# A probability turn that writes DRAM once and reads it back four times, with a longer pause before its use

## The chip, the cores and the metric

The kernel runs on one core of a Trainium2 chip. The metric is the device time of one execution in microseconds (us): the median of three runs is 922.42 us, from 922.07 to 927.72. The core has five engines that run their own instruction streams and meet through semaphores: TensorE (PE in the profile, PEld for its weight loads), VectorE (DVE), ScalarE (ACT), GpSimd (POOL) and SyncE (SP). In this kernel SP issues the loads of weights and POOL issues, beside a few small loads, the DMAs that this change is about.

## What is computed

Two layers over 256 positions of width 2048. Each layer multiplies x by one wide input matrix, runs three groups of heads side by side, gates them with SiLU, multiplies by an output matrix and applies a layer norm to the scaled residual:

```python
h = x @ w_in                              # 2048 -> 6672 columns
y_a = chunk_band_attention(q, k, v, rel)  # 8 "chunk" heads of 128, softmax over the chunks seen so far, with a bias by distance
o_b = gla_chunk_recurrence(...)           # 4 heads of gated linear attention
y_m = memory_attention(m_q, mk, mv)       # 4 "memory" heads, softmax over 256 fixed memory tokens
y   = concat(y_a * silu(a_z), y_b * silu(b_z), y_m * silu(m_z))
x   = layer_norm(alpha * x + y @ w_out)
```

Both softmax groups need their probabilities twice: the softmax is taken along the free dimension (one query position in each of the 128 partitions), but the product with the values wants the keys in the partitions. So each head's probabilities are turned (transposed) in between. The change is in this turn and in how long the program waits after it.

## The kernel before

**The stream of pieces.** Nearly all matmul work is a product of x (or of the gated heads) with a weight matrix of 512 (or 388) columns. Such a group is cut in 8 pieces. Each piece is loaded by SP into a tile `raw` (`piece`, L129), split by ACT into a rounded high part `wh` (L117) and by DVE into the rest `wl` (L118), and multiplied by PE in 16 matmuls (`ws_group`, weights stationary) or 12 (`as_group`, activations stationary), all recorded at L95 and accumulated in `acc`. `raw`, `wh` and `wl` have four buffers each, so the loads run up to about four pieces ahead of PE. A layer goes through its groups in a fixed order; the one that matters is, from the middle of the layer on: values 2, AQ0, AK0, values 3, AQ1, AK1, MQ, BZ, AZ0, AZ1, MZ, then four groups WO of the output matrix.

**Heads between pieces.** Every head is a Python generator (`a_head` L516 for the eight chunk heads, `m_head` L546 for the four memory heads, `gla` L312 for linear attention). After each piece the program calls `tick` (L52), which advances a count (by 1, or by 0.76 after a piece of 388 columns) and steps at most one generator that is due. A `yield 7` says: go on with me seven pieces later. At most two generators are active while linear attention runs, three afterwards. So the order of PE and of SP is written out by the program: a head's own matmuls stand at a fixed place between two pieces. DVE, ACT and POOL get their order from a scheduler that works with estimated times; each engine then executes strictly in its order.

**A chunk head** starts by asking for the bias of the head two further on (`load_bias`, L830, an SP load into one of four `bias` buffers; the buffer is free when the head four earlier has added its bias, L524). Then PE multiplies q and k (rows `bk<-qk,qk`), DVE scales and adds the bias (L524) and finds the maxima (L529), ACT takes the exponential (L531), DVE normalises (L532, L534), and `turned` (L505) turns the result: DVE transposes blocks of 32 by 32 (L508), which leaves the blocks in the wrong partitions; POOL writes them to a DRAM tile `home` with four DMAs (L511), one for every 32 partitions, each in pieces of one block row (96 numbers, 384 bytes), and reads `home` back with one DMA (L512) into `pT`. Then comes `yield 7`; PE multiplies `pT` with the values (rows `bk<-pT,asv`), ACT copies the result out (L543), and after `yield 2` the generator ends. The memory heads use the same `turned` with 128 numbers (512 bytes) to a piece; after their own `yield 7` ACT and DVE split `pT` (L117, L118), and two pieces later PE multiplies it with the memory's values (rows `bk<-sc,mv`).

A DMA from POOL is an instruction in POOL's stream: a read of `home` waits there until the writes have landed, and all that stands behind it on POOL waits too.

At the end of a group of gates the program calls `finish` (L69), which steps the heads that the gates need without further pieces, if they are not yet done.

Of the kernel before, what the change touches and what calls it, by code (L numbers as in the profile page):

```python
# [36 lines left out]
def hybrid_trunk_kernel(  # L37
# [7 lines left out]
    pe, dve, act, pool, sp = nc.tensor, nc.vector, nc.scalar, nc.gpsimd, nc.sync  # L45
# [44 lines left out]
    def nm(s):  # L90
        uid[0] += 1
        return f"{s}_{uid[0]}"

    def mm(o, l, r, start, stop):
        pe.matmul(o, l, r, start=start, stop=stop, skip_group_check=True)  # L95

    def bank():
        return psa.tile([P, 512], F32, name=nm("bk"), tag="bk")

    def scratch(shape, dtype=F32):  # L100
        return sc.tile(shape, dtype, name=nm("sc"), tag="sc")

    def small(shape, tag, bufs=1):
        return sm.tile(shape, F32, name=nm(tag), tag=tag, bufs=bufs)
# [400 lines left out]
    def turned(dst, src, n):  # L505

        blocks = scratch([P, 4, n])
        dve.transpose(blocks.rearrange("p b (g j) -> p g b j", j=32), src.rearrange("p (g b j) -> p g b j", b=4, j=32))  # L508
        home = drm.tile([P, 4, n], F32, name=nm("home"), tag=f"home{n}")
        for a in range(4):  # L510
            pool.dma_start(home[:, a].rearrange("(b i) n -> i b n", b=4), blocks[a * 32:(a + 1) * 32])  # L511
        pool.dma_start(dst, home)  # L512

    SCALE = P ** -0.5

    def a_head(h, load_bias, bias, q, k, asv, y):  # L516

        if h + 2 < 8:
            load_bias(h + 2)
        pb = bank()  # L520
        mm(pb[:, 0:128], q[:, 0:128], k[:, 0:128], True, True)
        mm(pb[:, 128:384], q[:, 128:256], k, True, True)
        s = scratch([P, 384])
        dve.scalar_tensor_tensor(s, pb[:, :384], SCALE, bias[h], op0=ALU.mult, op1=ALU.add)  # L524
        mx = small([P, 2], "mx", 4)
        zs = small([P, 2], "zs", 4)
        own = (slice(0, 128), slice(128, 384))
        for t in range(2):
            dve.tensor_reduce(mx[:, t:t + 1], s[:, own[t]], AX.X, ALU.max, negate=True)  # L529
        for t in range(2):  # L530
            act.activation(s[:, own[t]], s[:, own[t]], AF.Exp, bias=mx[:, t:t + 1], accum_out=zs[:, t:t + 1])  # L531
        dve.reciprocal(zs, zs)  # L532
        for t in range(2):
            dve.tensor_scalar(s[:, own[t]], s[:, own[t]], zs[:, t:t + 1], None, op0=ALU.mult)  # L534
        pT = tp.tile([P, 4, 96], F32, name=nm("pT"), tag="pT")
        turned(pT, s, 96)
        yield 7
        po = bank()
        v0 = 528 + h * P
        pv, pov = pT.rearrange("p a (g j) -> p g a j", j=32), po[:, :256].rearrange("p (t a j) -> p t a j", t=2, j=32)  # L540
        mm(pov, asv[:, 0, v0:v0 + P], pv[:, 0:2], True, False)
        mm(pov[:, 1], asv[:, 1, v0:v0 + P], pv[:, 2], False, True)
        act.copy(y, po[:, :256])  # L543
        yield 2

    def m_head(h, q, mk, mv, y):  # L546
# [17 lines left out]
        for t in range(2):  # L564
            dve.tensor_scalar(s[:, t], s[:, t], zs[:, t:t + 1], None, op0=ALU.mult)
        pT = hd.tile([P, 4, 128], F32, name=nm("pT"), tag="qe" if h % 2 else "gb_")
        turned(pT, s.rearrange("p t m -> p (t m)"), 128)
        yield 7
        ph, pl = scratch([P, 2, 256], F32R), scratch([P, 2, 256], F32R)
# [199 lines left out]
    for l in range(L):  # L769
# [58 lines left out]
        def load_bias(h):  # L828
            bias[h] = hd.tile([P, 384], F32, name=nm("bias"), tag="bias", bufs=4)
            sp.dma_start(bias[h], relw[l, h])  # L830
# [9 lines left out]
        for half in range(2):  # L840
            values(2 + half)
            q = heads(G_AQ0 if half == 0 else G_AQ1)
            k = heads(G_AK0 if half == 0 else G_AK1)
            gens.append([a_head(half * 4 + h, load_bias, bias, q[:, h], k[:, h], asv, yraw[1 + half][:, h]) for h in range(4)])
            waiting.extend(gens[-1])
# [36 lines left out]
        for n in range(WO_N):  # L882
            if last:
                g, b = scratch([P, 512]), scratch([P, 512])
            else:
                both = per.tile([P, 2, 512], F32, name=nm("gb"), tag=f"yr{n}")
                g, b = both[:, 0], both[:, 1]
# [126 lines left out]
```

## Time and profile before

| | before |
|---|---|
| median of three runs | 922.42 us (922.07 to 927.72) |
| profiled execution, its own time | 922.5 us |
| its span in the trace | 920.7 us |
| PE busy | 909.6 us, 99% of the span |
| DVE, ACT, POOL busy | 65%, 53%, 10% |
| DMAs of a turn | 4 writes `home<-sc` of 48 or 64 KB, 1 read `pT<-home` of 192 or 256 KB |
| turns in the program | 16 of chunk heads, 8 of memory heads |

The 1.8 us between the profiled execution's time and its span lie outside the recorded instructions. In the profile, times are counted from the start of the span. "Idle before" names what an engine waited for last. PE has almost no idle time, so what moves the end of this program is the little that PE does wait, and any new wait.

### The profile page before, as it was taken

The numbers are of one execution on the slowest core, as the hardware profiler recorded it, in microseconds if no ns is written. First come the engines' busy times: TensorE is split into PE (matmuls) and PEld (weight loads), VectorE is DVE, ScalarE is ACT, GpSimd is POOL, SyncE is SP. The second block draws the span as 40 slices with busy tenths as digits, with TensorE's granted clock in tenths as the row PEclk, the third lists the DMA queues.
The fourth block names the chain that finished last, engine by engine and source line by source line (L and its number), as shares of the span: only waits on it lengthen the run. The fifth ranks groups of instructions, "written<-read, shape, count | busy, mean of one in ns | idle before, by whom it ended". The sixth has DMA issues, their size and how long they took to land.

```text
span 920.7 us, 14332 instructions
## 1 busy us (share of the span) xinstructions
PE 909.6 (99%) x5420; PEld 798.8 (87%) x5420; DVE 602.2 (65%) x845; ACT 488.7 (53%) x702; POOL 87.8 (10%) x169
## 2 busy tenths in 40 slices
PE   9999999999999999999999999999989999999997
PEld 7889998998888888888888899889878888888885
DVE  6764478656566576555587665985746676776566
ACT  6644475475455565434476445654734565654350
POOL 1000000012033030000000000001211230310000
PEclk9999999999999999999999999999999999999998
DMA  9965865558576586655774466555565775776652
GB/s 306 335 191 173 297 219 165 157 178 278 170 216 203 200 252 205 216 195 184 233 255 164 152 205 202 186 163 179 209 212 175 220 214 177 228 251 208 199 162 91
DMA packets 75989, 189.33 MB, mean 206 GB/s; under 512 B 9224, under 2 KB 33160, under 8 KB 75664
## 3 DMA queue, kind: packets, MB, share of 16 engines
q1 hardware_dynamic: 69120, 173.30, 57.7%
q0 software_dynamic: 6656, 14.86, 5.5%
q8 instruction: 42, 0.69, 0.3%
q10 hardware_dynamic: 144, 0.26, 0.1%
q14 instruction: 27, 0.22, 0.1%
HBM read 181.01 MB, written 7.34 MB: 205 GB/s over the span
## 4 chain that ended last, share of the span: by engine, by line
PE 90%; DMA 4%; ACT 2%; DVE 1%; issue 1%; POOL 1%; SPq 0%; POOLq 0%
PE acc L95 82%; PE bk L95 7%; DMA home<-sc 2%; DMA raw<-w 2%; DMA pT<-home 1%; ACT wh L117 1%; POOL home L511 1%; ACT sc L474 1%; PE bk L599 0%; DVE wl L118 0%; ACT L290 0%; PE bk L498 0%; ACT asv L807 0%; DVE mx L529 0%; DVE qk L263 0%
## 5 line engine op out<-in xcount | busy, mean ns | idle before, releaser
L118 DVE TENSOR_TENSOR wl<-raw,wh 128x1024 fp32r<-128x1024 f32 (+3 forms) x321 | 369.9, 1154 | 251.6 <-ACT wh L117 250.3
L117 ACT CAST wh<-raw 128x1024 fp32r<-128x1024 f32 (+3 forms) x321 | 318.9, 995 | 338.1 <-PE acc L95 231.8
L95 PE MATMUL acc<-x,wh 128*128 128x512 f32 x1248 | 397.1, 400 | 0.2 <-ACT wh L117 0.2
L95 PE MATMUL acc<-wh,x 128*128 128x512 f32 (+2 forms) x1236 | 356.5, 369 | 0.0
L95 PEld LDWEIGHTS acc<-x,wl 128*128 128x128 f32 x1248 | 234.7, 188 | 55.3
L95 PEld LDWEIGHTS acc<-wh,x 128*128 128x128 f32 x1236 | 227.0, 188 | 27.8 <-ACT wh L117 0.4
L95 PE MATMUL acc<-x,wl 128*128 128x256 f32 x1248 | 246.0, 278 | 0.0
L95 PE MATMUL acc<-wl,x 128*128 128x512 f32 (+2 forms) x618 | 228.0, 369 | 0.0
L95 PEld LDWEIGHTS acc<-x,wh 128*128 128x128 f32 x1248 | 192.6, 189 | 2.5 <-ACT wh L117 0.8
L95 PEld LDWEIGHTS acc<-wl,x 128*128 128x128 f32 x618 | 116.0, 188 | 15.0 <-DVE wl L118 0.8
L511 POOL DMA_DIRECT2D home<-sc x96 | 52.5, 554 | 336.6 <-DVE sc L508 333.5
L531 ACT ACTIVATE sc<-sc,mx 128x128 f32<-128x128 f32 (+1 forms) x32 | 14.3, 448 | 10.6 <-DVE mx L529 10.5
L512 POOL DMA_DIRECT2D pT<-home x24 | 13.4, 560 | 54.2 <-DMA home<-sc 49.8
L95 PE MATMUL bk<-pT,asv 128*128 128x256 f32 (+1 forms) x64 | 14.0, 342 | 4.2 <-DMA pT<-home 4.2
L95 PEld LDWEIGHTS bk<-pT,asv 128*128 128x128 f32 x64 | 11.7, 197 | 5.9 <-DMA pT<-home 4.6
L386 ACT ACTIVATE sc<-sc 128x512 f32<-128x512 f32 x12 | 7.6, 633 | 15.4 <-DVE sc L384 15.3
L508 DVE STREAM_TRANSPOSE sc<-sc 128x384 f32<-128x384 f32 (+1 forms) x24 | 14.9, 621 | 0.6
L118 DVE TENSOR_TENSOR x<-sc,x 128x512 fp32r<-128x512 f32 x20 | 13.3, 684 | 0.7 <-ACT x L117 0.7
L304 POOL DMA_DIRECT2D gwraw<-gate_w x6 | 3.1, 522 | 106.0 <-PE bk L587 105.1
L95 PE MATMUL bk<-qk,qk 128*128 128x128 f32 (+1 forms) x64 | 13.1, 326 | 0.0
L118 DVE TENSOR_TENSOR x<-res,x 128x512 fp32r<-128x512 f32 (+2 forms) x14 | 10.4, 764 | 4.0 <-ACT x L117 4.0
L524 DVE SCALAR_TENSOR_TENSOR sc<-bk,bias 128x384 f32<-128x384 f32 x16 | 8.7, 543 | 6.6 <-PE bk L95 6.5
(207 smaller groups left out, 566.3 us busy)
## 6 DMA issues: line engine op xcount, KB each, us to landing
raw<-w SPq DMA_DIRECT2D x214, 512.0 KB, 4.3
raw<-w SPq DMA_DIRECT2D x64, 388.0 KB, 3.5
raw<-w SPq DMA_DIRECT2D x83, 256.0 KB, 3.5
bias<-relw SPq DMA_DIRECT2D x16, 192.0 KB, 4.2
home<-sc POOLq DMA_DIRECT2D x64, 48.0 KB, 3.7
pT<-home POOLq DMA_DIRECT2D x16, 192.0 KB, 4.1
res<-xT SPq DMA_DIRECT2D x4, 512.0 KB, 5.0
res<-xn SPq DMA_DIRECT2D x1, 2048.0 KB, 8.2
```

The lines of the kernel that those rows point to most:

```text
L95: pe.matmul(o, l, r, start=start, stop=stop, skip_group_check=True)
L117: act.copy(hi, src)
L118: dve.tensor_tensor(lo, src, hi.bitcast(F32), op=ALU.subtract)
L304: pool.dma_start(raw[i * 16:i * 16 + 16], gate_w[l])
L386: act.activation(dd, dd, AF.Abs)
L474: act.activation(sq, on[par][:, g], AF.Square, scale=1.0 / math.sqrt(P), accum_out=ms[:, par * 4 + g:par * 4 + g + 1])
L508: dve.transpose(blocks.rearrange("p b (g j) -> p g b j", j=32), src.rearrange("p (g b j) -> p g b j", b=4, j=32))
L511: pool.dma_start(home[:, a].rearrange("(b i) n -> i b n", b=4), blocks[a * 32:(a + 1) * 32])
L512: pool.dma_start(dst, home)
L524: dve.scalar_tensor_tensor(s, pb[:, :384], SCALE, bias[h], op0=ALU.mult, op1=ALU.add)
L531: act.activation(s[:, own[t]], s[:, own[t]], AF.Exp, bias=mx[:, t:t + 1], accum_out=zs[:, t:t + 1])
```

## The change

The one DRAM tile `home` keeps its size, but its rows are now the source's rows, unturned, so one DMA writes it; the blocks change partitions on the way back, where four DMAs each fill 32 partitions of `pT`. The pause of the chunk heads (not of the memory heads) is nine pieces.

```diff
@@ turned
         home = drm.tile([P, 4, n], F32, name=nm("home"), tag=f"home{n}")
-        for a in range(4):
-            pool.dma_start(home[:, a].rearrange("(b i) n -> i b n", b=4), blocks[a * 32:(a + 1) * 32])
-        pool.dma_start(dst, home)
+        pool.dma_start(home, blocks)
+        for b in range(4):
+            pool.dma_start(dst[b * 32:(b + 1) * 32], home[:, b].rearrange("(a i) n -> i a n", a=4))
@@ a_head
         turned(pT, s, 96)
-        yield 7
+        yield 9
         po = bank()
```

In the changed kernel the write has line L510 and the reads L512. Three places show what the change does to the order of the engines. The heads of a layer are numbered from 0.

POOL, first layer, the turns of chunk heads 0 and 1 (`home_1792` and `home_2065`) and what stands between them; minus is before, plus is the changed kernel:

```order
-L511 DMA home_1792<-sc_1790 32x4x96 x4
-L512 DMA pT_1789<-home_1792 128x384
+L510 DMA home_1792<-sc_1790 128x384
+L512 DMA pT_1789<-home_1792 32x4x96 x4
 L656 MEMSET gbrow_4341 128x128
 L658 DMA gbrow_4341<-ln_g 16x128
 L658 DMA gbrow_4341<-ln_b 16x128
-L511 DMA home_2065<-sc_2063 32x4x96 x4
-L512 DMA pT_2062<-home_2065 128x384
```

Five DMAs in either case; the single one is now the write.

PE, first layer, group AQ1. Before, head 0's product with the values (`pT_1789`) stands behind the group's second piece, and head 2's q times k (`bk_2121`) behind the third:

```order
L95 MATMUL bk_2093<-pT_1789,asv_729 128x256 [waits DMASW2_49,DVE_49]
L95 MATMUL bk_2093<-pT_1789,asv_729 128x128
L95 MATMUL acc_2012<-x_447,wh_2098 128x512 [waits Activation_49]
...
L95 MATMUL acc_2012<-x_447,wl_2099 128x256 x2
L95 MATMUL bk_2121<-qk_1497,qk_1215 128x128 [waits PE_49]
L95 MATMUL bk_2121<-qk_1497,qk_1215 128x256
```

In the changed kernel head 2's q times k stands behind the second piece (where `pT_1789` stood), and `pT_1789` two pieces later, behind the group's fourth piece and ahead of the next one (`acc_2168`):

```order
L95 MATMUL acc_2012<-x_513,wh_2141 128x512 x2
L95 MATMUL acc_2012<-x_513,wl_2142 128x256 x2
L95 MATMUL bk_2162<-pT_1789,asv_729 128x256 [waits DMASW2_49,DMASW1_49,DMASW7_49,DMASW0_49,PE_49]
L95 MATMUL bk_2162<-pT_1789,asv_729 128x128
L95 MATMUL acc_2168<-x_277,wh_2170 128x512 [waits Activation_49]
```

The product waits for four DMAs (DMASW) in place of one. Head 3's q times k, which stood one piece behind head 2's, now stands two pieces behind `pT_1789`, four behind head 2's. Between a chunk head's q times k and its product with the values there stand nine pieces, where seven stood (counting pieces of 388 columns for less).

SP, first layer, loads of the same group. Before, the load of head 5's bias (`bias_2166`, which waits until DVE has added head 1's bias) stands behind the group's fourth piece:

```order
L830 DMA bias_2119<-relw 128x384
L142 DMA raw_2144<-w 128x1024 [waits DMAHW6_49,DVE_49]
L830 DMA bias_2166<-relw 128x384 [waits DVE_49]
L142 DMA raw_2194<-w 128x1024 [waits DMAHW7_49,Activation_49]
L142 DMA raw_2216<-w 128x1024 [waits DMAHW1_49,Activation_49]
```

In the changed kernel the same load (`bias_2213`) stands two pieces later:

```order
L830 DMA bias_2093<-relw 128x384
L142 DMA raw_2118<-w 128x1024 [waits DMAHW5_49,DVE_49]
L142 DMA raw_2140<-w 128x1024 [waits DMAHW6_49,DVE_49]
L142 DMA raw_2169<-w 128x1024 [waits DMAHW7_49,DVE_49]
L142 DMA raw_2191<-w 128x1024 [waits DMAHW1_49,DVE_49]
L830 DMA bias_2213<-relw 128x384 [waits DVE_49]
```

## Prediction, made before the result was known

> **What bounds the kernel now.** The first part of the page comes first: who is busy.
>
> ```profile
> PE 909.6 (99%) x5420; PEld 798.8 (87%) x5420; DVE 602.2 (65%) x845; ACT 488.7 (53%) x702; POOL 87.8 (10%) x169
> ```
>
> PE is idle for 920.7 - 909.6 = 11.1 us of the span. An edit that leaves the number of matmuls alone can win no more than these 11.1 us and whatever PE loses by running slow; everything else it does is hidden or a loss. The table of waits, for PE alone, says what the idle time is:
>
> ```profile
> PE bk L95 <- DMA pT<-home: 4.2, 2, 2.8
> PE bk L95 <- DVE eps L768: 1.1, 1, 1.1
> ```
>
> Two waits for turned probabilities take 4.2 us, the longer 2.8 us; the rest of the 11.1 us is the start and the end of the program. The timeline of PE shows which heads these are. First the first layer, heads 1 to 3, up to head 4's q times k; then the same end in the second layer:
>
> ```profile
> 196.72 0.82 PE L95 MATMUL bk<-qk,qk 128*128 128x128 f32 x4
> 200.16 0.81 PE L95 MATMUL bk<-pT,asv 128*128 128x256 f32 x4
> 203.60 0.82 PE L95 MATMUL bk<-qk,qk 128*128 128x128 f32 x4
> 207.04 0.82 PE L95 MATMUL bk<-qk,qk 128*128 128x128 f32 x4
> 218.84 0.81 PE L95 MATMUL bk<-pT,asv 128*128 128x256 f32 x4
> 225.08 0.81 PE L95 MATMUL bk<-pT,asv 128*128 128x256 f32 x4
> 230.08 0.92 PE L95 MATMUL bk<-pT,asv 128*128 128x256 f32 x4 [1.40 <-DMA pT<-home]
> 247.58 0.82 PE L95 MATMUL bk<-qk,qk 128*128 128x128 f32 x4
> ...
> 677.42 0.81 PE L95 MATMUL bk<-pT,asv 128*128 128x256 f32 x4
> 683.81 1.65 PE L95 MATMUL bk<-pT,asv 128*128 128x256 f32 x4 [2.78 <-DMA pT<-home]
> 702.63 0.81 PE L95 MATMUL bk<-qk,qk 128*128 128x128 f32 x4
> ```
>
> The late one is head 3 in both layers. Its product took 1.65 us the second time, twice what the others take, and the windows around it say why: PEclk, the granted clock, is 0.57 in the 4 us that follow the longer wait, and 1.00 on either side.
>
> ```profile
> 680.00:683.00 3.00, 1.03 (x7) 0.73 (x5) 1.09 (x1) 1.04 (x1) 0.00 (x0) 1.00 0.99 328
> 683.00:687.00 4.00, 3.19 (x10) 2.78 (x11) 0.13 (x1) 0.37 (x1) 0.00 (x0) 0.57 0.52 172
> 687.00:690.00 3.00, 3.00 (x19) 2.60 (x19) 0.25 (x1) 1.33 (x2) 0.00 (x0) 1.00 0.00 0
> ```
>
> **What the two waits cost together.** From 196.72 to 207.04 PE takes three equal steps of 3.44 us, each one piece and one head's products. From 218.84 to 225.08 are two pieces and one such product, 6.24 us, so a piece alone is 6.24 - 3.44 = 2.80. In the first layer head 3's product was due at 225.08 + 3.44 = 228.52 and came at 230.08, 1.56 late; its row is 0.92 instead of 0.81, so 0.11 more. From there to head 4's q times k is 247.58 - 230.08 = 17.50, undisturbed 17.39. An undisturbed stretch from head 2's product to head 4's q times k is then 3.44 + 17.39 = 20.83. It took 22.50 in the first layer, 1.67 too long, and 702.63 - 677.42 = 25.21 in the second, 4.38 too long (2.95 late, 1.43 for the half clock). Together **6.05 us**.
>
> **Why head 3 is late.** POOL's timeline:
>
> ```profile
> 203.43 2.21 POOL L511 DMA_DIRECT2D home<-sc  x4 [12.61 <-DVE sc L508]
> 208.59 0.56 POOL L512 DMA_DIRECT2D pT<-home  x1 [2.94 <-DMA home<-sc]
> 212.66 2.18 POOL L511 DMA_DIRECT2D home<-sc  x4 [3.50 <-DVE sc L508]
> 218.92 0.56 POOL L512 DMA_DIRECT2D pT<-home  x1 [4.08 <-DMA home<-sc]
> 219.47 2.18 POOL L511 DMA_DIRECT2D home<-sc  x4
> 226.60 0.56 POOL L512 DMA_DIRECT2D pT<-home  x1 [4.95 <-DMA home<-sc]
> ```
>
> Head 3 began on PE one step behind head 2 (207.04 against 203.60), but a turn holds POOL for 219.47 - 212.66 = 6.81 us, most of it waiting for the writes to land. Head 3's first write has no idle time before it: it queued behind head 2's read.
>
> **The DMAs turned about: 0.** The page's list of DMA issues (KB each, then us to landing):
>
> ```profile
> home<-sc POOLq DMA_DIRECT2D x64, 48.0 KB, 3.7
> pT<-home POOLq DMA_DIRECT2D x16, 192.0 KB, 4.1
> home<-sc POOLq DMA_DIRECT2D x32, 64.0 KB, 4.1
> pT<-home POOLq DMA_DIRECT2D x8, 256.0 KB, 5.2
> ```
>
> One issue on POOL is 2.21 / 4 = 0.55, by either row. A chunk head's turn was: last of four writes issued after 3 x 0.55, landed after 3.7, read landed after 4.1: 9.45 us. It becomes one write of 192 KB, then three issues, then the last of four reads of 48 KB. Nothing in the trace writes 192 KB to `home` or reads 48 KB from it, so I take the same sizes in the other direction: 4.1 + 1.65 + 3.7 = 9.45. POOL is held as long as before, in another order: 0.55 and the wait, then four issues. Lower and upper bounds of the two unknown landings, by the fastest and the slowest of all turn DMAs:
>
> ```profile
> DMA to landing us min/median/max: 1.9/3.8/5.6
> ```
>
> That makes a turn 1.9 + 1.65 + 1.9 = 5.45 to 5.6 + 1.65 + 5.6 = 12.85 us, 4.0 shorter to 3.4 longer. What covers the longer end is weighed next, head by head.
>
> **The pause of nine pieces: -6.05 us.** Two more pieces give every chunk head 2 x 2.80 = 5.6 us. The worst was 2.95 late, so even with nothing else changed it has 5.6 - 2.95 = 2.65 us to spare. But head 3 also starts later: head 2 moves one step up, to 200.16; head 0's product follows two pieces later (200.16 + 3.44 + 2.80 = 206.40) and head 3 two more pieces on, near 212.6. It is then some 12.4 us behind head 2 where it was 3.44, more than the 6.81 that a turn holds POOL, so it no longer queues. Heads 1 and 2 are now one step apart and head 2 queues behind head 1; it had its product at 225.08, two us after its read should have landed (218.92 + 4.1 = 223.0), and the 5.6 us cover 6.81 - 3.44 = 3.4 of queueing. So I expect no wait for `pT` by a chunk head, even at the 3.4 longer turn for most of them, and without a wait no half clock. What is late next on PE: nothing that the wait table shows; the pieces.
>
> **Weights: 0.** SP's stream moves too. Before, SP stood still ahead of AQ1's fifth piece, because the bias of head 5 needs DVE's L524 of head 1:
>
> ```profile
> 185.27 0.34 SPq L142 DMA_DIRECT2D raw<-w  x1
> 198.55 0.33 SPq L830 DMA_DIRECT2D bias<-relw  x1
> 203.25 1.05 ACT L117 CAST wh<-raw 128x1024 fp32r<-128x1024 f32 x1 [1.35 <-DMA raw<-w]
> 207.51 0.81 PE L95 MATMUL acc<-x,wh 128*128 128x512 f32 x2
> ```
>
> That fifth piece was rounded at 203.25 + 1.05 = 204.30 and used at 207.51: 3.2 us of cover, the thinnest place of the stretch. The bias load now stands two pieces later in SP's order while head 1's L524 stays where it was, so SP stands still for less and the cover grows. If DVE's new order (head 2's softmax sits closer to head 1's) ate that cover, each us beyond 3.2 would be a us of PE.
>
> **Memory heads: 0.** Their pause is the same. The last two of the first layer:
>
> ```profile
> 343.87 0.76 DVE L118 TENSOR_TENSOR sc<-pT,sc 128x256 fp32r<-128x256 f32 x2 [0.24 <-ACT sc L117]
> 349.66 0.88 PE L95 MATMUL bk<-sc,mv 128*128 128x256 f32 x6
> ```
>
> `pT` is split at 344.63 and used at 349.66: 5.0 us of cover against at most 3.4. ACT and DVE would stand behind a late `pT` and hold up the next pieces, which have some us of cover of their own.
>
> **Three more semaphores for each product: 0.** Sixteen products now wait for four DMAs. In the step from 200.16 the product waited for a DMA and for DVE, and the step is 3.44, the same as that of q times k, so a further wait has no visible price. The nearest row for an upper end is a whole product of four matmuls in 0.81, 0.2 each: 16 x 3 x 0.2 = 9.6 us if each wait cost as much as a matmul. I take 0, as that step shows, and keep part of it in the range.
>
> **The sum.** 922.5 (the profiled execution's own time, 0.1 from the median) - 6.05 = **916.5 us**, 0.7% less. A difference under 1% is about what a measurement of this kernel can't tell from none.
>
> **A rule that speaks against part of it.** The Trainium skill, "TensorE: Matmul & The Clock Gate", section "HAM oscillation — how this bites in real kernels", says that only idle gaps above some 3.4 us make the clock drop. By that rule a 2.8 us wait has no such cost, the half clock has another cause and stays, and the sum is that of the first rival below. The trace speaks against it: the clock is 0.57 only in the 4 us behind the longest wait, and behind the 1.40 us wait the product took 0.92, not 1.65.
>
> **The rivals.**
> 1. *The half clock is not the wait's and stays.* Then only the lateness goes: 6.05 - 1.43 = 4.6, 917.9 us. For it: the shorter wait had none. Against it: the place. 0.07.
> 2. *A wait stays or a new one comes,* for `pT`, for the semaphores or for AQ1's weights, and takes part of the gain: 917.9 to 922.5. For it: the pauses shift every head's DVE and ACT work against the pieces. Against it: 2.65 and 3.2 us of cover. 0.11.
> 3. *Slower: the four reads run one after another.* If the reads of a turn don't overlap, the last lands after 4.1 + 4 x 3.7 = 18.9 in place of 9.45. The memory heads have 5.0 us of cover; 9.45 - 5.0 = 4.4 late, once for each pair, four pairs, each with a half clock of 1.43: 4 x 5.9 = 23.5, so 916.5 + 23.5 = 940 us. It decides from 5.0 us of extra landing, and outweighs the gain from 6.5 (4 x 1.5 = 6). Against it: four writes, issued 0.55 apart, let POOL go on 4.08 us after the last issue ended, so these overlapped. With smaller extra landings, 922.5 to 931: 0.05; beyond 931.7: 0.05.
> 4. *More than 1% faster.* That needs 9.2 us out of 11.1 of idle time and the half clock; the start and end are not touched. 0.02.
>
> **How the numbers follow.** The forecast, 916.5 with 0.8 on either side, has 0.70. 915.5 to 922.0 adds rival 1 and nearly all of rival 2, and leaves out some 0.15 above and 0.03 below. Faster by over 1%: 0.02; within 1%: 0.70 + 0.07 + 0.11 + 0.05 = 0.93; slower by over 1%: 0.05.
>
> **What would show it.** The two rows `PE bk L95 <- DMA pT<-home` are gone from the table of PE's waits; PE's idle time is near 6.9 us; the clock is 1.00 through the second layer's AK1; the single write lands in some 4 us and POOL's reads show no long wait but the first; SP's wait at L830 shrinks from 12.9. It is wrong if PE waits for `pT` again, if `acc` rows wait for ACT or DVE by more than a few tenths of a us, or if the `sc<-pT` casts wait several us each.

## The result, and the profile after

| | before | after |
|---|---|---|
| median of six runs each | 923.15 us (922.07 to 927.72) | 916.58 us (916.03 to 917.06) |
| profiled execution, its own time | 922.5 us | 916.47 us |
| its span | 920.7 us | 914.7 us |

The ratio after to before is 0.992, with a 95% interval of 0.990 to 0.994: a gain of 0.8% by the ratio and of 0.7% by the two medians. It lies within the 1% named above, and still the interval is clear of no change. The changed kernel's six runs lie within 1.0 us of each other; those of before within 5.7.

The page of the changed kernel, its first part:

```profile
span 914.7 us, 14341 instructions
...
PE 907.3 (99%) x5420; PEld 797.9 (87%) x5420; DVE 601.3 (66%) x845; ACT 492.2 (54%) x706; POOL 87.8 (10%) x169
```

PE is idle for 914.7 - 907.3 = 7.4 us, where it was idle for 11.1. Its table of waits (us in total, times, longest) has no row for `pT` any more, and begins so (what follows is 0.3 us and less):

```profile
PE bk L95 <- DVE eps L768: 1.1, 1, 1.1
PE acc L95 <- ACT wh L117: 0.6, 2, 0.3
```

PE's timeline, first from head 1's q times k to head 4's in the first layer, then the end of the same stretch in the second layer:

```profile
196.83 0.81 PE L95 MATMUL bk<-qk,qk 128*128 128x128 f32 x4
200.27 0.82 PE L95 MATMUL bk<-qk,qk 128*128 128x128 f32 x4
206.50 0.81 PE L95 MATMUL bk<-pT,asv 128*128 128x256 f32 x4
212.73 0.82 PE L95 MATMUL bk<-qk,qk 128*128 128x128 f32 x4
224.53 0.81 PE L95 MATMUL bk<-pT,asv 128*128 128x256 f32 x4
227.98 0.81 PE L95 MATMUL bk<-pT,asv 128*128 128x256 f32 x4
239.78 0.81 PE L95 MATMUL bk<-pT,asv 128*128 128x256 f32 x4
246.01 0.82 PE L95 MATMUL bk<-qk,qk 128*128 128x128 f32 x4
...
690.46 0.81 PE L95 MATMUL bk<-pT,asv 128*128 128x256 f32 x4
696.69 0.82 PE L95 MATMUL bk<-qk,qk 128*128 128x128 f32 x4
```

Every product takes 0.81 and none has idle time before it. Head 4's q times k comes at 246.01 where it came at 247.58, and in the second layer at 696.69 where it came at 702.63: 5.94 us earlier, of the 6.0 us by which the span is shorter. The 4 us of the second layer that ran at a clock of 0.57 now run at 1.00:

```profile
683.00:687.00 4.00, 4.00 (x25) 3.48 (x24) 2.89 (x3) 1.66 (x3) 0.00 (x0) 1.00 0.55 201
```

POOL's timeline, the turns of heads 1, 2 and 3 in the first layer (one write and four reads each):

```profile
205.33 0.56 POOL L510 DMA_DIRECT2D home<-sc  x1 [14.86 <-DVE sc L508]
207.79 2.19 POOL L512 DMA_DIRECT2D pT<-home  x4 [1.89 <-DMA home<-sc]
210.93 0.56 POOL L510 DMA_DIRECT2D home<-sc  x1 [0.95 <-DVE sc L508]
216.30 2.17 POOL L512 DMA_DIRECT2D pT<-home  x4 [4.80 <-DMA home<-sc]
218.46 0.56 POOL L510 DMA_DIRECT2D home<-sc  x1
222.42 2.17 POOL L512 DMA_DIRECT2D pT<-home  x4 [3.39 <-PE acc L95]
```

Head 3's write still has no idle time before it: it queues behind head 2's reads. How long it queues, DVE's rows for head 3's transpose tell, first in the kernel before, then in the changed one:

```profile
216.28 0.58 DVE L508 STREAM_TRANSPOSE sc<-sc 128x384 f32<-128x384 f32 x1
```

```profile
217.31 0.58 DVE L508 STREAM_TRANSPOSE sc<-sc 128x384 f32<-128x384 f32 x1
```

Before, the blocks were ready at 216.86 and the first write began at 219.47, 2.6 us later (3.1 in the second layer); now they are ready at 217.89 and the write begins at 218.46, 0.6 us later (0.3). Head 3's last read is issued by 222.42 + 2.17 = 224.59 and its product comes at 239.78, 15.2 us later. The list of DMA issues (KB each, median us to landing):

```profile
home<-sc POOLq DMA_DIRECT2D x16, 192.0 KB, 2.7
pT<-home POOLq DMA_DIRECT2D x64, 48.0 KB, 4.0
```

By these medians, a chunk head's turn is 2.7 + 3 x 0.55 + 4.0 = 8.35 us where it was 9.45. A single landing can differ much from the median: head 2's write in the first layer took 5.1 us.

### The profile page after: what moved, and what is told of

Same layout as the page of the kernel before. It is cut to its first block, busy times and chain, and to the rows that moved or that the text cites. A ratio compares the mean times of both kernels' runs of the same rounds, so it can differ in the third digit from the quotient of the medians.

```text
span 914.7 us, 14341 instructions
## 1 busy us (share of the span) xinstructions
PE 907.3 (99%) x5420; PEld 797.9 (87%) x5420; DVE 601.3 (66%) x845; ACT 492.2 (54%) x706; POOL 87.8 (10%) x169
## 4 chain that ended last, share of the span: by engine, by line
PE 98%; DMA 1%; SPq 0%; DVE 0%; ACT 0%; issue 0%
PE acc L95 90%; PE bk L95 7%; DMA raw<-w 1%; PE bk L599 0%; PE bk L498 0%; SPq L165 0%; SPq L178 0%; PE bk L397 0%; SPq L180 0%; ACT res L755 0%; ACT wh L117 0%; DVE stats L740 0%; PE bk L344 0%; DVE res L739 0%; DVE res L691 0%
## 5 line engine op out<-in xcount | busy, mean ns | idle before, releaser
L512 POOL DMA_DIRECT2D pT<-home x96 | 52.4, 553 | 56.7 <-DMA home<-sc 24.3
L510 POOL DMA_DIRECT2D home<-sc x24 | 13.4, 560 | 358.4 <-DVE sc L508 352.9
L632 DVE SCALAR_TENSOR_TENSOR res<-res,acc 128x512 f32<-128x512 f32 x15 | 9.7, 684 | 5.1 <-PE acc L95 5.1
```

The lines of the kernel that those rows point to most:

```text
L510: pool.dma_start(home, blocks)
L512: pool.dma_start(dst[b * 32:(b + 1) * 32], home[:, b].rearrange("(a i) n -> i a n", a=4))
L632: dve.scalar_tensor_tensor(r, r, ALPHA, acc, op0=ALU.mult, op1=ALU.add)
```

## The experiments

**Is it the pause or the turned DMAs?** First the pause alone, with the DMAs of before, then the DMAs alone, with the pause of seven.

```diff
-        yield 7
+        yield 9
```

> The pause of nine pieces alone; the turn writes DRAM four times and reads it once, as before. Theory 'the pause does it all': no wait of PE for pT, 6.0 us less than the kernel before, 916.5 us, as the full change. Theory 'the turned DMAs have a share': PE still waits for pT somewhere, or the time lies above the full change by 1 us or more, 917.5 to 920. If three more semaphores at each product cost PE something, this kernel (one semaphore) is faster than the full change, by up to 9.6 us; I expect 0.

Measured: 916.66 us (916.08 to 916.98, ten runs), ratio 0.993 (0.990 to 0.996). PE has no wait for `pT`. The pause alone gives the whole gain. It also prices the four semaphores of a product: with one DMA to wait for the kernel takes 916.66, with four 916.58, so the three further waits cost nothing that can be measured.

```diff
-        for a in range(4):
-            pool.dma_start(home[:, a].rearrange("(b i) n -> i b n", b=4), blocks[a * 32:(a + 1) * 32])
-        pool.dma_start(dst, home)
+        pool.dma_start(home, blocks)
+        for b in range(4):
+            pool.dma_start(dst[b * 32:(b + 1) * 32], home[:, b].rearrange("(a i) n -> i a n", a=4))
```

> The turned DMAs alone, with the pause of seven pieces. 'The pause does it all': head 3 stays late in both layers, 922.5 us, within 0.7 of the kernel before. 'The turned DMAs have a share': the profile of the full change has the 192 KB write landed after 2.7 us and the 48 KB reads after 4.0, so a turn takes 2.7 + 1.65 + 4.0 = 8.35 in place of 9.45; 1.1 us come off the lateness in each layer (1.56 and 2.95), 920.3 us, and 918.9 if the half clock goes with it.

Measured: 924.21 us (919.96 to 932.47, twelve runs), ratio 1.001 (0.998 to 1.004). The turned DMAs alone are worth nothing that these runs can tell: the interval reaches from 0.2% faster to 0.4% slower. This kernel's PE waits for `pT` in the same two places as before, the second time for 3.7 us instead of 2.8; first its row of waits, then POOL's rows for head 3, first layer:

```profile
PE bk L95 <- DMA pT<-home: 5.1, 2, 3.7
```

```profile
219.95 0.56 POOL L510 DMA_DIRECT2D home<-sc  x1
224.88 2.18 POOL L512 DMA_DIRECT2D pT<-home  x4 [4.37 <-DMA home<-sc]
```

The reads may start at 224.88, 1.7 us sooner than the one read of before (226.60), but there are four of them: the last has been issued at 224.88 + 2.18 = 227.06, against 226.60 + 0.56 = 227.16. What the single write saves ahead of the wait, three more issues take behind it. In the second layer the reads start only 0.3 us sooner (678.68 against 679.01), so the last is issued 1.3 us later (680.86 against 679.57), and the product is later too.

**How much pause is needed?** Eight and six pieces, with the DMAs of before, and eleven in the changed kernel.

```diff
-        yield 7
+        yield 8
```

> A pause of eight pieces, DMAs as before. Two reasons for the gain are told apart by the size: the pause gives each head 2.80 us a piece, and it moves the places where heads start. By the first alone head 3 of the second layer stays 2.95 - 2.80 = 0.15 us late and the first layer is on time: 916.7. If the starts matter, PE's order decides: here head 3's q times k stands three pieces behind head 2's where it stood one behind, so it does not queue on POOL, has several us of cover, and the time is again 916.5, with no wait for pT at all in the table.

Measured: 916.73 us (916.09 to 917.38, ten runs), ratio 0.993 (0.991 to 0.995). One more piece is enough. POOL and PE of this kernel, head 3 in the first layer:

```profile
217.20 2.21 POOL L511 DMA_DIRECT2D home<-sc  x4
223.65 0.56 POOL L512 DMA_DIRECT2D pT<-home  x1 [4.25 <-DMA home<-sc]
```

```profile
234.34 0.81 PE L95 MATMUL bk<-pT,asv 128*128 128x256 f32 x4
```

Head 3 still queues on POOL (no idle time before its write), but from the end of its read's issue, 224.21, to its product are 10.13 us. In the kernel before, it had 228.52 - 227.16 = 1.36 until its product was due. Of the 8.8 us more, 2.8 are the further piece; 3.0 come from head 3's later place (its q times k at 210.07, where it was at 207.04), and 2.95 from POOL, whose queue ahead of head 3 ends sooner (the read is issued by 224.21 instead of 227.16), since head 2 has moved up a step (its q times k at 200.40, where it was at 203.60).

```diff
-        yield 7
+        yield 6
```

> A pause of six pieces, DMAs as before: heads 1, 2 and 3 then start one step (3.44 us) apart and queue on POOL, 6.81 us each. Head 3's read should land some 4 us after its place on PE, in both layers. If a wait of that length halves the clock for 3.4 us, each layer loses 4 + 1.4 us over an undisturbed 916.5: 927.3 us, with the granted clock under 1 behind the wait in both layers. If the half clock of the kernel before was not the wait's, it shows in none or at another place, and the time is near 924.5.

Measured: 933.26 us (931.41 to 936.03, four runs), ratio 1.011 (1.007 to 1.016). Slower, as expected, by more than expected (927.3). Five products wait; PE's rows for them:

```profile
225.10 0.92 PE L95 MATMUL bk<-pT,asv 128*128 128x256 f32 x4 [1.07 <-DMA pT<-home]
231.50 0.92 PE L95 MATMUL bk<-pT,asv 128*128 128x256 f32 x4 [2.68 <-DMA pT<-home]
683.04 0.92 PE L95 MATMUL bk<-pT,asv 128*128 128x256 f32 x4 [1.19 <-DMA pT<-home]
689.64 1.03 PE L95 MATMUL bk<-pT,asv 128*128 128x256 f32 x4 [2.90 <-DMA pT<-home]
762.05 1.62 PE L95 MATMUL bk<-pT,asv 128*128 128x256 f32 x4 [2.94 <-DMA pT<-home]
```

The windows behind the three long waits (granted clock third from the end of a row):

```profile
232.00:237.00 5.00, 5.00 (x21) 4.29 (x21) 0.00 (x0) 0.81 (x2) 0.00 (x0) 0.66 0.42 142
...
690.00:694.00 4.00, 4.00 (x16) 3.46 (x15) 0.00 (x0) 0.37 (x1) 0.00 (x0) 0.57 0.48 170
...
762.00:766.00 4.00, 3.95 (x14) 3.42 (x15) 1.25 (x2) 0.79 (x2) 1.12 (x2) 0.57 0.79 264
```

A drop of the clock follows each wait of 2.68 us and more and none of the two shorter ones. The expectation had counted on the heads that were late before; the wait at 762.05 is that of another, later head, which had no wait at seven pieces.

```diff
-        yield 9
+        yield 11
```

> The full change with a pause of eleven pieces. If all of the gain is the wait that went, two pieces more are worth nothing: 916.6 us. If a longer pause makes the memory heads or the last gates late, PE waits there and the time is above 917.5.

Measured: 916.46 us (916.12 to 916.78, four runs), ratio 0.992 (0.991 to 0.994): the same as with nine. Beyond eight pieces nothing more is to be had.

**Is it the queue on POOL that made head 3 late?** The kernel before, with its pause of seven, but with head 3 alone begun later:

```diff
     def a_head(h):
+        if h == 3:
+            yield 2
```

> Kernel before, with one edit: chunk head 3 of each layer starts two pieces later. Its pause and that of all others stays at seven pieces, the DMAs stay as before. Theory 'head 3 was late because it queued on POOL behind head 2': the queue (6.81 - 3.44 = 3.4 us) is gone, head 3 is on time, no wait for pT, 916.6 us. Theory 'seven pieces are too short for a turn': head 3 waits as before, 922.5.

Measured: 917.32 us (916.35 to 917.78, four runs), ratio 0.993 (0.992 to 0.995). Nearly the whole gain, without a longer pause for any head. POOL of this kernel, head 3 in the first layer:

```profile
218.85 2.20 POOL L511 DMA_DIRECT2D home<-sc  x4 [1.37 <-DVE sc L508]
```

Its first write now waits for DVE's transpose and not for POOL. Its q times k starts 6.4 us later than in the kernel before (213.40 against 207.04), and its first write all the same 0.6 us earlier (218.85 against 219.47). Seven pieces suffice for a head that does not queue; the lateness was that of one head that began one step behind another.

**What do the turned DMAs do for the memory heads?** The memory heads' pause is shortened to five pieces, in the changed kernel and in the kernel with the pause of nine and the DMAs of before.

```diff
     def m_head(h):
...
-        yield 7
+        yield 5
```

> The full change, and the memory heads' pause cut from seven pieces to five, 5.6 us less. It takes the cover away that hides the turned DMAs there. In the profile of the full change the second parts of the probabilities were ready 4.1 to 10.3 us ahead of the product that uses them; less 5.6 leaves one head 1.5 late and one 0.1: 918.2 us. If the four reads were much slower than one, more heads would wait, above 920.

> The same cut of the memory heads' pause, with the chunk heads' pause of nine pieces and the old DMAs (four writes, one read). With these DMAs the parts were ready 5.5 to 9.9 us ahead; less 5.6 leaves two heads 0.1 late: 916.8 us. If the DMAs turned about cost or save nothing, this and the kernel with turned DMAs and the same pauses lie within 1 us of each other; if turned DMAs are slower for the memory heads, this one is faster by 1 to 3 us.

Measured: 919.61 us (918.61 to 919.82, four runs), ratio 0.996 (0.994 to 0.997), with the turned DMAs; 927.64 us (925.13 to 930.65, eight runs), ratio 1.005 (1.003 to 1.007), with those of before. The first expectation missed by 1.4 us, the second by 11. Here, where the cover has been cut away, the kernel with the turned DMAs is 8.0 us the faster one. With the turned DMAs the shorter pause costs 919.61 - 916.58 = 3.0 us: in the profiled execution PE is idle for 0.9 us more and busy for 2.4 us more than in the changed kernel, without a drop of the clock. Row by row, PE is 0.4 us behind the changed kernel from the start of the program on, where the clock rose 1.0 us later, and loses another 2.8 around the four pairs of memory heads. PE's waits, first with the turned DMAs, then with those of before:

```profile
PE bk L95 <- ACT sc L117: 1.0, 2, 0.5
```

```profile
PE bk L95 <- ACT sc L117: 6.2, 3, 3.1
PE bk L95 <- DVE sc L118: 1.6, 2, 0.8
```

POOL's timelines for the first two memory heads of the first layer, turned DMAs first; the first row of each is the second head's write or writes, the next the first head's read or reads:

```profile
298.04 0.56 POOL L510 DMA_DIRECT2D home<-sc  x1 [2.01 <-DMA home<-sc]
298.83 2.21 POOL L512 DMA_DIRECT2D pT<-home  x4 [0.23 <-issue]
```

```profile
297.75 2.18 POOL L511 DMA_DIRECT2D home<-sc  x4 [0.32 <-DVE sc L508]
301.72 0.56 POOL L512 DMA_DIRECT2D pT<-home  x1 [1.79 <-DMA home<-sc]
```

With the DMAs of before, the first head's read stands behind the second head's four writes, 2.18 us of POOL, and starts 2.9 us later. But POOL had issued these writes by 299.93 and was then idle for 1.79 us, until writes had landed: it was not the issue of the four writes that held this read. Nor is the read what PE waited for here. It landed 4.0 us after its issue, at 305.7, and ACT's casts of it began at 308.45, without idle time, behind the cast of a piece:

```profile
308.45 1.33 ACT L117 CAST sc<-pT 128x256 fp32r<-128x256 f32 x4
```

With the turned DMAs the first of these casts stands ahead of that piece's cast, at 306.09. Another of the three waits for ACT is of the same kind (1.56 us at 806.00: the read had landed at 803.6, the cast began at 805.24 behind a piece's). Only the longest, 3.14 us, goes back to a cast that waited for its read, which took 6.0 us to land. So two of the waits point to the order that the scheduler gave ACT, and one to a landing. No run takes these apart: that the form of the DMAs itself makes the 8.0 us isn't shown, and how they divide stays open.

**Is the half clock the wait's?** In the kernel before, 14 products of the identity with itself are put ahead of head 3's product, into columns of its bank that nothing else uses, so that PE has work while it would wait:

```diff
         po = bank()
+        if h == 3:
+            for _ in range(14):
+                mm(po[:, 256:384], ident, ident, True, True)
```

> The kernel before, with 14 idle matmuls (identity times identity, 128 columns, 28 rows of 0.107 us, some 3.0 us) put ahead of head 3's product with the values in each layer; their result is used nowhere. PE is then busy where it waited, and the wait becomes shorter or goes. Theory 'the half clock comes from PE standing still': no granted clock under 1 between start and end, and every execution takes 916.6 + 2 x 3.0 = 922.6 us, plus what is left of a wait, within a us or two, although no work was saved. If the half clock and the spread of the kernel before (918.8 to 929.7) have another cause, they stay: a spread of 5 us or more, and a profile with a stretch at 0.5.

Measured: 923.04 us (922.57 to 923.89, twelve runs), ratio 1.001 (0.999 to 1.003); the kernel before ran from 917.05 to 925.32 beside it. PE's timeline and the windows of the second layer:

```profile
682.54 3.29 PE L95 MATMUL bk<-ident 128*128 128x128 f32 x28
```

```profile
683.00:687.00 4.00, 4.00 (x32) 3.72 (x31) 1.23 (x1) 0.77 (x2) 0.00 (x0) 1.00 0.78 267
```

The filler takes 3.29 us in each layer, 6.6 in all, which is what it stands above the kernels without the wait (923.04 - 916.6 = 6.4). The clock is 1.00 all the way, and the spread of the runs is 1.3 us where that of before is 8.3. With PE busy, neither the half clock nor the spread appears: both come from PE standing idle.

## Why the prediction was right

The forecast was 916.5; the median is 916.58 and the profiled execution's own time 916.47. Step by step:

- **The two waits, 6.05 us.** Right in sum: the own time fell by 6.03. Right in its parts too: the rows for `pT` are gone, PE's idle time is 7.4 (6.9 was named), the clock is 1.00 where it was 0.57. But the 6.05 is that of one execution. The kernel before took 918.84 to 929.74 in 27 runs, and the share of the half clock in it differs from one run to the next (below); that this execution lay at the median was known, that it stood for the others was not.
- **The cause, POOL's queue.** Shown: moving head 3 alone gives nearly all of the gain, and the queue, 2.6 us in the first layer and 3.1 in the second, is longer than the lateness of 1.56 and 2.95 that it had to explain.
- **The pause, -6.05.** Shown: the pause alone gives 916.66. Of the two reasons given, the first, more cover for every head, holds by its size: from head 3's q times k to its product are 27.05 us, where 21.48 were due before, 5.6 more. No run lengthens the pause without moving the heads, so it isn't shown alone. The second does not, for the reason given: head 3's q times k came at 212.73, as worked out ("near 212.6"), but head 3 still queues on POOL, if only for 0.6 us where it was 2.6, since head 2's reads go out only at 216.30, after a wait of 4.80 for its write, and hold POOL until 218.47. The step "so it no longer queues" failed: it set the distance of two q times k against the time of a turn, but head 2's write came 10.7 us after its q times k and head 3's blocks were ready 5.2 us after theirs. Nor did head 2 queue behind head 1: its write waited 0.95 us for DVE. The 15.2 us between head 3's last read and its product make all this harmless.
- **The turned DMAs, 0.** Shown, by the kernel that has them alone. The reason held as well: the same time on POOL in another order. The landings were sized a little off: the single write 2.7 (4.1 assumed), the reads 4.0 (3.7), a turn of 8.35 rather than 9.45. One of the signs named did not come: that POOL's reads would show no long wait but the first. Those of heads 2 and 3 wait 4.80 and 3.39 us, without harm to PE.
- **Weights, 0.** Right. SP's row and the two rows that tell the cover of AQ1's fifth piece, in the changed kernel:

```profile
SPq L830 <- DVE sc L524: 15.8, 2, 7.9
```

```profile
196.88 1.03 ACT L117 CAST wh<-raw 128x1024 fp32r<-128x1024 f32 x1
...
207.07 0.71 PE L95 MATMUL acc<-x,wh 128*128 128x512 f32 x2
```

  SP stands still for 7.9 us at the longest where it was 12.9, and the fifth piece has 207.07 - 197.91 = 9.2 us of cover where it had 3.2.
- **Memory heads, 0.** Right in the result, thin in the working. The prediction read the cover of one head, 5.0 us; over the eight memory heads of the kernel before, the time from DVE's second part to the product goes from 5.8 down to none at all, in the second layer. The quoted head was no bound for the others. In the changed kernel the least is that of the second layer's last memory head:

```profile
805.77 0.76 DVE L118 TENSOR_TENSOR sc<-pT,sc 128x256 fp32r<-128x256 f32 x2 [1.87 <-ACT sc L117]
...
810.66 0.88 PE L95 MATMUL bk<-sc,mv 128*128 128x256 f32 x6
```

  It ends at 806.53 and is used at 810.66, 4.1 us later. That the cover grew was not foreseen: more of ACT's time goes into waiting (two `sc<-pT` casts of sixteen wait 2.9 and 2.7 us for `pT`, where the longest was 1.1, which comes near a sign that was named for being wrong), without an effect on PE. With this cover cut to five pieces the kernels with the two forms of DMAs differ by 8.0 us, so "0" holds for this pause and not for every one.
- **Semaphores, 0.** Shown, by 916.66 against 916.58.
- **The rivals.** The first, a half clock that is not the wait's, falls: the filler removes it, and in the kernel with six pieces it follows three more waits. With it falls, for this case, the rule quoted from the Trainium skill, "TensorE: Matmul & The Clock Gate", section "HAM oscillation — how this bites in real kernels", that only gaps above some 3.4 us matter: waits of 2.68 to 2.94 us were enough. The third, reads that run one after another, falls with the landings: the 64 reads land in 4.0 us each at the median, issued 0.55 apart. A new wait (the second) did not come: `acc` waits for `wh` by 0.6 us in all, the longest 0.3. Nor did a gain of over 1% (the fourth).

## What to carry to other kernels

Where one engine's stream both starts a DMA and waits for an earlier one (here POOL, 6.8 us a turn), two users that begin closer together than that queue, and the wait shows up with the second of them. Moving that one user, or giving its result one more piece of time, was worth as much as a longer pause for all, while a cheaper form of the DMAs behind the same order was worth nothing. And a forecast made from one execution should be held against the spread of the runs: this kernel, whose time differed by more than 1% from run to run while that of its neighbours without the wait differed by less than 0.2%, had something in it, a wait and a clock that drops after it, that the one profile shows once.

## What the runs showed of the hardware

**The clock drops after less idle time than expected, in steps of 3.41 us.** In the traces of the kernel before and of those with a pause of six and with the memory heads' pause of five and the DMAs of before, the clock is either 1.00 or 0.50 between start and end, and each stretch at 0.50 is 3.413 us long. The distances between them are whole multiples of that: in the kernel before 679.25 us (199 times) from the clock's first rise to the drop, with six pieces 228.69 us (67 times). The Trainium skill, "TensorE: Matmul & The Clock Gate", section "What's actually happening", says that a free-running window of 3413 ns decides; the traces agree. So what counts is how much of one such window is idle. Counted in such windows from the clock's rise, PE was busy for 16 to 43% of the seven that a drop followed (one in the kernel before, one with the turned DMAs alone, three with six pieces, two with the memory heads' five and the DMAs of before), and for 56% and more of all others away from the program's start and end. Waits of 2.68 us and more dropped it in these profiles, single waits of 1.40 and less did not. In the kernel with the memory heads' pause of five and the DMAs of before, a window with two shorter waits in it, of 1.56 and 0.82 us, was enough, while two of 1.52 and 0.82 in its first layer were not: they fell otherwise into the windows. The window of the first layer, then that of the drop and the next one:

```profile
308.53:311.94 3.41, 1.91 (x11) 1.62 (x12) 3.17 (x6) 2.29 (x8) 0.00 (x0) 1.00 0.63 192
...
803.50:806.90 3.40, 1.43 (x9) 0.94 (x7) 1.85 (x4) 1.94 (x4) 0.00 (x0) 1.00 0.84 301
806.90:810.30 3.40, 2.98 (x10) 2.70 (x11) 2.35 (x6) 1.84 (x5) 0.00 (x0) 0.50 0.51 160
```

In the first layer PE is busy for 1.91 of 3.41 us, and the clock stays at 1.00 in the next window too; in the second it is busy for 1.43 of 3.40 us, and the clock of the next 3.4 us is 0.50.

**It has a part in the spread.** Of 27 runs of the kernel before, beside the first experiments, those with a mean granted clock of 0.997 to 0.999 took 918.8 to 921.6 us, those with 0.995 or 0.996 took 921.8 to 925.8, those with 0.993 or 0.994 took 924.9 to 929.4, and the one with 0.991 took 929.7. In the 17 runs of it beside the filler the groups overlap: 918.5 to 924.1 with 0.997, 922.6 to 925.3 with 0.996. The half clock can't be all of it: a stretch of 3.413 us at 0.50 costs at most 1.7 us and takes 0.002 off the mean clock, so from 0.997 to 0.991 it accounts for some 5 us where the times lie 8 to 11 apart. The rest would be waits of different length, which the single trace can't show.

The kernels in which PE does not wait there (the changed one, and those with the pause of nine alone, of eight, and of eleven) lie between 916.0 and 917.4 in all their runs, and the one with the filler, idle nowhere between start and end, within 1.3 us. So both parts go with PE's idle time.
